# Hybrid encoder trunk on one core: gate and branch products with tokens on the partitions, and rounded activations and remainder in one 512-column step

## The chip, the cores and the metric

The kernel runs on one core of one Trainium2 chip. The metric is the device time in microseconds of one execution. The median of three runs of the kernel before is 993.6 us.

## The reference

Two layers work on 256 tokens of 1024 channels, all in float32. Each layer takes three mixers of the same input (differential attention, a gated DeltaNet scanned in both directions, windowed attention), gates and sums them, and then runs a gated feed-forward stage:

```python
z = x @ w_in                                   # gz: 3 x 1024 gate columns among them
proj = jnp.einsum('btnc,ncd->btnd', ys, w_branch)      # ys: three mixers, 512 wide
gates = jax.nn.sigmoid(gz.reshape(B, T, N_BRANCHES, D))
merged = jnp.sum(gates * proj, axis=2)
h = merged @ w_out;  x = layer_norm(DEEPNORM_ALPHA * x + h, ...)
gate, up = jnp.split(x @ w_up, 2, axis=-1)     # 2 x 2816 columns
gate = dwconv_centred(gate, conv_w) + conv_b   # width 3 over the tokens
f = (jax.nn.silu(gate) * up) @ w_down;  x = layer_norm(DEEPNORM_ALPHA * x + f, ...)
```

## The kernel before

**Three products for one.** TensorE multiplies in a rounded form of float32 (`F32R`). To keep the precision, each operand is split into a rounded part and a remainder (hi and lo), and `mm3` takes three products of each pair of tiles: hi*hi, hi*lo, lo*hi. The activations lie in `xTh` (rounded) and `xTl` (remainder), 8 tiles of 128 channels by 256 tokens each. The weights come from HBM in blocks of 512 KB (`raw`, 128x1024), ScalarE rounds a block (`hi`), VectorE takes the remainder (`lo`); `weights` and `take` do that, with 4 buffers of each kind.

**Two layouts.** `proj_ch` (and `pair`, which calls it) puts output channels on the partitions: the weights are stationary, the activations stream by, 256 columns in a step; a block of 128 output channels takes 8 x 3 steps of 256 columns. `token_major` and `proj_tok` put tokens on the partitions: the activations are stationary and 512 weight columns stream by. Before, the gates (`gz`, 24 blocks of 128 channels a layer), the branch products (`wb`, 12 blocks of 256 channels a layer), the feed-forward gate (`fg`, 22 blocks) and up (`fu`, 18 blocks) are of the first kind. `merge.product` makes the gates and branch products: a gate goes through Tanh on ScalarE, VectorE multiplies it with the branch product (`g_product<-g_product,mm_product`), adds the three branches, and splits the sum into hi and lo (`mh`, `ml`), which are stationary in `proj_tok("wo", ...)`.

**The feed-forward stage** goes over 11 groups `c` of 256 channels. A group makes `pg = pair("fg", l, c)` in one bank of PSUM, convolves it over the tokens (one affine step on ScalarE and two steps on VectorE for each of the two halves, read from PSUM), takes Silu, multiplies with `pu` (also in PSUM) and splits the result for `proj_tok("fd", ...)`. PSUM has 4 banks for such products (`mm`), 2 for the DeltaNet chain (`ch`), 2 for attention (`at`).

**The order** of the work is made at build time: `Plan` records all instructions with their dependencies, and a list scheduler with a table of costs sets the order on every engine. `ORDER` lists for each layer the products in the order in which they are asked for, `PRIO` shifts priorities. The gates and branch products stand in `ORDER` as fillers between the steps of the mixers. PE, VectorE and ScalarE each keep the order that results; a waiting instruction holds up all behind it on its engine.

Of the kernel before, what the change touches and what calls it, by code (L numbers as in the profile page):

```python
# [10 lines left out]
F32 = mybir.dt.float32  # L11
F32R = mybir.dt.float32r
F16 = mybir.dt.float16
U8 = mybir.dt.uint8
AF = mybir.ActivationFunctionType
# [35 lines left out]
PIECES = 2  # L51
PAIRS = ("s", "yc")
KEEP = {'wo': (4, ('D', 'N', 'x')), 'fd': ((4, ('g', 'g')), (4, ('g', 'g')))}
ORDER = [[('av', 0), ('ab', 0), ('k', 0), ('ak', 0), ('gz', 10), ('aq', 0), ('k', 1), ('q', 0), ('aq', 1), ('q', 1), ('ak', 1), ('gz', 1), ('v', 0), ('v', 1), ('gz', 0), ('gate', 0), ('gate', 1), ('cq', 0), ('wb', 1), ('ckv', 0), ('gz', 11), ('gz', 2), ('gz', 3), ('wb', 0), ('cq', 1), ('wb', 2), ('wb', 3), ('gz', 9), ('wb', 9), ('gz', 4), ('wb', 11), ('gz', 5), ('gz', 6), ('wb', 10), ('gz', 7), ('wb', 4), ('gz', 8), ('wb', 6), ('wb', 7), ('wb', 8), ('wb', 5)], [('av', 0), ('ab', 0), ('k', 0), ('ak', 0), ('gz', 10), ('aq', 0), ('k', 1), ('q', 0), ('aq', 1), ('q', 1), ('ak', 1), ('v', 1), ('gz', 0), ('gz', 3), ('v', 0), ('gate', 0), ('gate', 1), ('ckv', 0), ('gz', 1), ('cq', 0), ('wb', 1), ('wb', 0), ('gz', 11), ('gz', 2), ('cq', 1), ('wb', 2), ('gz', 9), ('wb', 3), ('gz', 4), ('wb', 9), ('wb', 11), ('gz', 5), ('gz', 6), ('wb', 10), ('wb', 4), ('gz', 8), ('gz', 7), ('wb', 6), ('wb', 7), ('wb', 8), ('wb', 5)]]


SIZES = {F32: 4, F32R: 4, F16: 2, U8: 1}
# [376 lines left out]
def _blocks(depth=DEPTH):  # L434
# [6 lines left out]
    for l in range(depth):  # L441
# [10 lines left out]
        for n in (0, 2, 1):  # L452
            for m in range(4):
                for b in range(2):
                    cols(("gz", l * 3 + n, 2 * m + b), "w_in", l, 4368 + n * D + (2 * m + b) * P, P)
                if n != 2:
                    cols(("wb", l, n, m), "w_branch", l, m * 256, 256, 4, sub=(n,))
                else:
                    sel = np.concatenate([g * 256 + t * 64 + np.arange(64) for t in range(4) for g in range(2)])
                    out.append((("wb", l, n, m), 4, 256, lambda i, l=l, m=m, sel=sel: i["w_branch"][l, 2][sel, m * 256:(m + 1) * 256]))  # L460
# [34 lines left out]
def tile_encoder_trunk(ctx: ExitStack, tc: tile.TileContext, a: dict, out: bass.AP, depth=DEPTH, tap=None):  # L495
# [884 lines left out]
    def merge(l, pr, ys, mh, ml):  # L1380
        gates, macc = {}, {}

        def product(nme, b):
# [18 lines left out]
            if nme != "wb":  # L1402
                return pair(nme, l, b)
# [102 lines left out]
```

## Time and profile before

| | |
|---|---|
| median of 3 runs | 993.6 us (992.38 to 994.38) |
| profiled execution, its time | 992.73 us |
| profiled execution, its span | 991.0 us |
| PE busy | 969.0 us (98%) |
| PE weight loads busy | 906.2 us (91%) |
| VectorE (DVE) busy | 722.3 us (73%) |
| ScalarE (ACT) busy | 588.8 us (59%) |
| GpSimd (POOL) busy | 73.0 us (7%) |
| mean HBM traffic | 166 GB/s |
| mean granted TensorE clock | 0.997 of full speed |

The span runs from the first to the last instruction; the execution's own time has 1.7 us more around it. Matmuls overlap: each record of a matmul is longer than the distance to the next one, and the sum of the records is more than the span, so the cost of a step is read from how many start in a stretch, not from its mean duration. A line of kernel.py is L195 for all instructions, as the recorder issues them, so rows are told apart by the names of tiles.

### The profile page before, as it was taken

How to read it: one execution, taken by the hardware profiler on the slowest of the kernel's cores; microseconds unless marked ns; L12 is line 12 of the kernel's file. 1: busy time of each engine (PE TensorE's matmuls, PEld its weight loads, DVE VectorE, ACT ScalarE, POOL GpSimd, SP SyncE). 2: the span in 40 equal slices, each digit the busy share in tenths (PEclk: the TensorE clock that was granted, in tenths of full speed). 3: DMA queues.
4: the chain of work that ended last, by engine and by line, in shares of the span. 5: the costliest groups of instructions: out<-in, count | busy, mean ns of one | idle time of the engine just before them, and what ended most of it. 6: DMA issues, size and time to landing. Idle time of an engine off the chain costs nothing.

```text
span 991.0 us, 19154 instructions
## 1 busy us (share of the span) xinstructions
PE 969.0 (98%) x7598; PEld 906.2 (91%) x7598; DVE 722.3 (73%) x1310; ACT 588.8 (59%) x1068; POOL 73.0 (7%) x84
## 2 busy tenths in 40 slices
PE   7999999999999999999999999999999999999996
PEld 6899999989988999988889999999899799999885
DVE  6799786665689766665688996966756995667555
ACT  5868966664455655553557787757744654555441
POOL 0520010100000100000005200000000010000000
PEclk9999999999999999999999999999999999999998
DMA  7644355464575655555635543425445855555661
GB/s 266 187 153 147 102 148 145 144 182 138 178 248 168 203 187 186 172 175 188 213 104 158 165 121 115 146 81 176 154 137 181 273 190 159 191 180 188 196 191 42
DMA packets 50109, 165.43 MB, mean 167 GB/s; under 512 B 5751, under 2 KB 11271, under 8 KB 50020
## 3 DMA queue, kind: packets, MB, share of 16 engines
q1 hardware_dynamic: 48644, 159.78, 50.9%
q0 software_dynamic: 1376, 4.43, 1.5%
q8 instruction: 59, 0.97, 0.4%
q14 instruction: 30, 0.25, 0.1%
HBM read 163.12 MB, written 1.07 MB: 166 GB/s over the span
## 4 chain that ended last, share of the span: by engine, by line
PE 81%; DVE 6%; ACT 4%; DMA 2%; POOL 1%; issue 1%; POOLq 0%; DVEq 0%; ACTq 0%
PE mm_proj_ch L195 48%; PE ch_run L195 6%; PE mm_product L195 6%; PE mm_run L195 6%; PE mm_token_major L195 3%; PE at_window L195 2%; PE at_attention L195 2%; PE ch_solve L195 2%; DMA raw_proj_tok<-in_w_dram 2%; PE ch_gdn L195 1%; ACT hi_take L195 1%; PE ch_scan L195 1%; DMA raw_take<-in_w_dram 1%; PE ch_finish L195 1%; POOL x_decay L195 1%
## 5 line engine op out<-in xcount | busy, mean ns | idle before, releaser
L195 PE MATMUL mm_proj_ch<-xTh,hi_take 128*128 128x256 f32 x1488 | 421.8, 286 | 0.9 <-ACT hi_take L195 0.5
L195 PE MATMUL mm_proj_ch<-xTl,hi_take 128*128 128x256 f32 x1488 | 420.2, 285 | 0.0
L195 PE MATMUL mm_proj_ch<-xTh,lo_take 128*128 128x256 f32 x1488 | 419.1, 285 | 0.0
L195 DVE TENSOR_TENSOR lo_take<-raw_take,hi_take 128x1024 fp32r<-128x1024 f32 x219 | 266.8, 1232 | 104.5 <-ACT hi_take L195 86.4
L195 ACT ACTIVATE hi_take<-raw_take 128x1024 fp32r<-128x1024 f32 x214 | 224.4, 1057 | 195.0 <-PE mm_proj_ch L195 136.5
L195 PEld LDWEIGHTS mm_proj_ch<-xTh,hi_take 128*128 128x128 f32 x1488 | 280.2, 189 | 3.5 <-ACT hi_take L195 1.8
L195 PEld LDWEIGHTS mm_proj_ch<-xTh,lo_take 128*128 128x128 f32 x1488 | 279.5, 189 | 2.8 <-issue 1.6
L195 PEld LDWEIGHTS mm_proj_ch<-xTl,hi_take 128*128 128x128 f32 x1488 | 280.2, 189 | 1.6 <-issue 0.8
L195 ACT ACTIVATE hi_proj_tok<-raw_proj_tok 128x1024 fp32r<-128x1024 f32 x50 | 52.8, 1060 | 66.8 <-PE mm_run L195 37.9
L195 DVE TENSOR_TENSOR lo_proj_tok<-raw_proj_tok,hi_proj_tok 128x1024 fp32r<-128x1024 f32 x50 | 61.0, 1223 | 42.9 <-ACT hi_proj_tok L195 42.9
L195 DVE SCALAR_TENSOR_TENSOR z_conv_silu<-mm_proj_ch,col_params,z_conv_silu 128x254 f32<-128x254 f32 (+1 forms) x96 | 39.1, 474 | 0.6 <-ACT z_conv_silu L195 0.5
L195 DVE SCALAR_TENSOR_TENSOR g_product<-g_product,mm_product 128x512 f32<-128x512 f32 x24 | 16.5, 686 | 24.5 <-PE mm_product L195 24.5
L195 POOL TENSOR_TENSOR s_tail<-s_tail,nhalf 128x1 f32<-128x1 f32 x8 | 5.3, 665 | 380.4 <-DVE s_tail L195 380.4
L195 ACT ACTIVATE e_window<-e_window,s_window 128x256 f32<-128x256 f32 x55 | 26.5, 498 | 10.5 <-DVE s_window L195 10.4
L195 PEld LDWEIGHTS <-h_solve 128*128 128x128 f16 x640 | 25.8, 98 | 4.2 <-ACT h_solve L195 0.4
L195 PE MATMUL mm_run<-hi_proj_tok,tile_encoder_trunk 128*128 128x512 f32 x88 | 27.5, 392 | 1.6 <-ACT tile_encoder_trunk L195 1.2
L195 PE MATMUL mm_run<-hi_proj_tok,ile_encoder_trunk 128*128 128x512 f32 x88 | 27.3, 391 | 0.0
L195 ACT ACTIVATE e_attention<-e_attention,s_attention 128x256 f32<-128x256 f32 x46 | 22.7, 503 | 5.3 <-DVE s_attention L195 5.1
L195 PE MATMUL mm_product<-ya_attention,hi_take 128*128 128x256 f32 x128 | 25.1, 287 | 0.0
L195 PE MATMUL mm_product<-ya_gdn,hi_take 128*128 128x256 f32 x128 | 23.7, 283 | 0.0
L195 PE MATMUL mm_product<-yc_window,hi_take 128*128 128x256 f32 x128 | 23.7, 283 | 0.0
L195 ACT ACTIVATE tile_encoder_trunk<-tile_encoder_trunk 128x512 f32<-128x512 f32 (+1 forms) x22 | 13.6, 625 | 16.6 <-DVE tile_encoder_trunk L195 16.6
(348 smaller groups left out, 1656.0 us busy)
## 6 DMA issues: line engine op xcount, KB each, us to landing
raw_take<-in_w_dram SPq DMA_DIRECT2D x226, 512.0 KB, 4.2
raw_proj_tok<-in_w_dram SPq DMA_DIRECT2D x60, 512.0 KB, 4.0
G_load_G<-band SPq DMA_DIRECT2D x24, 192.0 KB, 3.5
ya_ln_params<-in_lnp_dram POOLq DMA_DIRECT2D x16, 256.0 KB, 5.9
x<-in_xT_dram SPq DMA_DIRECT2D x4, 256.0 KB, 4.5
x<-in_x_dram SPq DMA_DIRECT2D x2, 512.0 KB, 4.6
out_dram<-x SPq DMA_DIRECT2D x8, 128.0 KB, 1.8
_tile_encoder_trunk<-in_w_dram SPq DMA_DIRECT2D x4, 128.0 KB, 3.7
```

Of the source, the lines that this page charges most:

```text
L195: op.ways.append((eng, lambda fn=fn, args=args, kw=kw: fn(*args, **kw), _cost(eng, name, outs, ins, args, kw), table))
```

## The change

It does four things. (1) The gate and branch weights are stored as blocks of 256 input rows by 512 output columns, and `merge.product` puts tokens on the partitions: the activations (or a mixer's output) are stationary and 512 weight columns stream by, for two halves of the tokens (`tt`) at once in two banks. (2) The gated sum then has tokens on the partitions, and four 128x128 transposes for each of 4 quarters a layer turn it back before it is split. (3) `xTh` and `xTl` become two halves of one tile `xT`, so that `wide` takes the steps hi*xTh and hi*xTl as one step of 512 columns; the two halves of the result are added afterwards by `halves_sum` (a copy by ScalarE or VectorE, and an addition on VectorE) into a buffer in SBUF, from which the rest of the stage reads. `wide` is used for `fg` and `fu` only. (4) `PRIO` and `ORDER` are new: `ORDER` has 6 gate and 6 product entries a layer instead of 12 and 12 (the long lists are left out below).

```diff
@@ _blocks
         for n in (0, 2, 1):
-            for m in range(4):
+            for h in range(2):
+                for b in range(KD // 2):
+                    cols(("gz", l * 3 + n, h, b), "w_in", l, 4368 + n * D + h * 512, 512, 2, b * 2)
                 for b in range(2):
-                    cols(("gz", l * 3 + n, 2 * m + b), "w_in", l, 4368 + n * D + (2 * m + b) * P, P)
-                if n != 2:
-                    cols(("wb", l, n, m), "w_branch", l, m * 256, 256, 4, sub=(n,))
...
+                    if n != 2:
+                        cols(("wb", l * 3 + n, h, b), "w_branch", l, h * 512, 512, 2, b * 2, sub=(n,))
...
-    xTh = cp.tile([P, KD, T], F32R, name="xTh")
-    xTl = cp.tile([P, KD, T], F32R, name="xTl")
+    xT = cp.tile([P, KD, 2, T], F32R, name="xT")
+    xTh, xTl = xT[:, :, 0], xT[:, :, 1]
...
+    def wide(key):
+
+        ps = ps_mm((P, 2, T))
+        hi, lo = take(key)
+        for j in range(KD):
+            TE.matmul(ps, hi[j], xT[:, j], start=j == 0, stop=False)
+            TE.matmul(ps[:, 0], lo[j], xTh[:, j], start=False, stop=j == KD - 1)
+        return ps
+
+    def halves_sum(out, ps):
+        A.copy(out, ps[:, 1])
+        V.tensor_tensor(out, ps[:, 0], out, op=ALU.add)
@@ merge.product
+            n, h = divmod(b, 2)
+            nk = KD if nme == "gz" else 4
+            pss = [ps_mm() for _ in range(2)]
+            for c in range(nk // 2):
+                w = take((nme, l * 3 + n, h, c if nme == "gz" else 1 - c))
+                for tt in range(2):
+                    ts = slice(tt * P, (tt + 1) * P)
+                    for j in range(2):
+                        if nme == "gz":
+                            lh, ll = xTh[:, 2 * c + j, ts], xTl[:, 2 * c + j, ts]
+                        else:
+                            lh, ll = [y[1 - c][:, j, ts] for y in ys[n]]
+                        mm3(pss[tt], lh, ll, w[0][j], w[1][j], c == j == 0, 2 * c + j == nk - 1)
             if nme == "gz":
-                n, m = divmod(b, 4)
-                ps = pair("gz", l * 3 + n, m)
-                gates[b] = buf("g", (P, 2, T))
-                S.activation(gates[b], ps, AF.Tanh, scale=0.5)
+                gates[b] = [buf("g") for _ in range(2)]
+                for tt in range(2):
+                    S.activation(gates[b][tt], pss[tt], AF.Tanh, scale=0.5)
                 return None
...
-                for j in (3, 2, 1, 0):
-                    mm3(ps[:, c], hi[j][:, cs], lo[j][:, cs], yh[j // 2][:, j % 2], yl[j // 2][:, j % 2], j == 3, j == 0)
...
+            for tt, gt in enumerate(gates.pop(b)):
+                V.scalar_tensor_tensor(gt, gt, 1.0, pss[tt], ALU.add, ALU.mult)
+                parts = macc.setdefault((h, tt), [])
+                parts.append(gt)
+                if len(parts) > 1:
+                    V.tensor_tensor(parts[0], parts[0], gt, op=ALU.add)
+                if len(parts) == 3:
+                    ps = ps_at((P, 4, P))
+                    for k in range(4):
+                        TE.transpose(ps[:, k], parts[0][:, k * P:(k + 1) * P], ident)
+                    h_, l_ = [buf(("z", "kk")[h], (P, 4, P), F32R) for _ in range(2)]
+                    S.activation(h_, ps, AF.Copy, scale=0.5)
+                    V.scalar_tensor_tensor(l_, ps, 0.5, h_.bitcast(F32), ALU.mult, ALU.subtract)
+                    mh[h, tt], ml[h, tt] = h_, l_
@@ feed-forward stage
-            pg = pair("fg", l, c)
+            pg = buf("h16", (P, 2, T))
+            for i in range(2):
+                ps = wide(("fg", l, 2 * c + i))
+                halves_sum(pg[:, i], ps)
...
-                pu = pair("fu", l, c)
+                pu = buf("h16", (P, 2, T))
+                for i in range(2):
+                    ps = wide(("fu", l, 2 * c + i))
+                    halves_sum(pu[:, i], ps)
```

**Place 1, PE in the feed-forward stage of the first layer.** `mm_proj_ch` and `mm_wide` are products in PSUM, `xTh`, `xTl` and `xT` the activations, `hi_take` and `lo_take` a weight block. Before, around the start of a new `fg` product:

```order
L195 MATMUL mm_proj_ch_33_804<-xTl,hi_take_81_809 128x256
L195 MATMUL mm_proj_ch_36_830<-xTh,hi_take_86_832 128x256
L195 MATMUL mm_proj_ch_36_830<-xTl,hi_take_86_832 128x256
L195 MATMUL mm_proj_ch_33_804<-xTh,lo_take_81_810 128x256
L195 MATMUL mm_proj_ch_33_804<-xTh,hi_take_81_809 128x256
```

With the change, at such a place:

```order
L195 MATMUL mm_wide_8_801<-xT,hi_take_77_803 128x512
L195 MATMUL mm_wide_8_801<-xT,lo_take_77_804 128x256
L195 MATMUL mm_wide_11_818<-xT,hi_take_80_820 128x512
L195 MATMUL mm_wide_13_829<-xT,hi_take_82_831 128x512
L195 MATMUL mm_wide_13_829<-xT,lo_take_82_832 128x256
```

Three steps of 256 columns became one of 512 and one of 256; each product now fills a bank of its own, and a second one is still begun before the first has its remainder of the weights.

**Place 2, VectorE at the same stage, one group of four weight blocks.** `e_...` is the convolved gate, `h_...` the new buffer of the added halves. Before:

```order
L195 TENSOR_TENSOR lo_take_101_895<-raw_take_104_893,hi_take_101_894 128x1024
L195 SCALAR_TENSOR_TENSOR e_tile_encoder_trunk_7_888<-mm_proj_ch_42_881,col_params_1_93,e_tile_encoder_trunk_7_888 128x255 x2
L195 TENSOR_TENSOR lo_take_102_901<-raw_take_105_899,hi_take_102_900 128x1024
L195 TENSOR_TENSOR lo_take_103_904<-raw_take_106_902,hi_take_103_903 128x1024
L195 TENSOR_TENSOR lo_take_104_909<-raw_take_107_907,hi_take_104_908 128x1024
L195 TENSOR_TENSOR e_tile_encoder_trunk_6_871<-mm_proj_ch_41_872,e_tile_encoder_trunk_6_871 128x512
L195 TENSOR_TENSOR N_tile_encoder_trunk_4_880<-e_tile_encoder_trunk_6_871,N_tile_encoder_trunk_3_879 128x512
```

With the change:

```order
L195 TENSOR_TENSOR lo_take_92_884<-raw_take_95_882,hi_take_92_883 128x1024
L195 TENSOR_TENSOR h_tile_encoder_trunk_7_870<-mm_wide_21_871,h_tile_encoder_trunk_7_870 128x256
L195 TENSOR_TENSOR D_tile_encoder_trunk_2_848<-e_tile_encoder_trunk_3_837,D_tile_encoder_trunk_1_847 128x512
L195 SCALAR_TENSOR_TENSOR e_tile_encoder_trunk_5_879<-h_tile_encoder_trunk_7_870,col_params_1_92,e_tile_encoder_trunk_5_879 128x255 x2
L195 TENSOR_TENSOR lo_take_93_888<-raw_take_96_886,hi_take_93_887 128x1024
L195 TENSOR_TENSOR h_tile_encoder_trunk_7_870<-mm_wide_22_875,h_tile_encoder_trunk_7_870 128x256
L195 TENSOR_TENSOR lo_take_94_895<-raw_take_97_893,hi_take_94_894 128x1024
L195 TENSOR_TENSOR h_tile_encoder_trunk_4_859<-mm_wide_19_860,h_tile_encoder_trunk_4_859 128x256
L195 TENSOR_TENSOR lo_take_95_899<-raw_take_98_897,hi_take_95_898 128x1024
L195 TENSOR_TENSOR h_tile_encoder_trunk_4_859<-mm_wide_20_864,h_tile_encoder_trunk_4_859 128x256
L195 TENSOR_TENSOR e_tile_encoder_trunk_4_858<-h_tile_encoder_trunk_4_859,e_tile_encoder_trunk_4_858 128x512
```

Behind each weight block there is one more addition of 128x256, and the convolution reads SBUF. Of the 80 copies that go before these additions, 73 stand on ScalarE and 7 on VectorE.

**Place 3, PE at the end of the first layer's mixers.** `mm_product` is a branch product, `mm_run` the first output projection (`wo`), `at_product` the new transposes, `tri` the identity. Before:

```order
L195 MATMUL mm_product_10_662<-ya_gdn_1_451,hi_take_66_660 128x256
L195 MATMUL mm_run_1_686<-hi_proj_tok_1_684,z_product_1_669 128x512
L195 MATMUL mm_run_1_686<-lo_proj_tok_1_685,z_product_1_669 128x512
L195 MATMUL mm_run_2_687<-hi_proj_tok_1_684,z_product_1_669 128x512
L195 MATMUL mm_run_2_687<-lo_proj_tok_1_685,z_product_1_669 128x512
L195 MATMUL mm_product_10_662<-ya_gdn_1_449,lo_take_66_661 128x256
```

With the change:

```order
L195 MATMUL mm_product_24_667<-hi_take_68_672,ya_gdn_1_458 128x512
L195 MATMUL mm_run_1_689<-hi_proj_tok_1_687,z_product_1_661 128x512
L195 MATMUL mm_run_1_689<-lo_proj_tok_1_688,z_product_1_661 128x512
L195 MATMUL mm_run_1_689<-hi_proj_tok_1_687,z_product_2_662 128x512
L195 MATMUL mm_run_2_690<-hi_proj_tok_1_687,z_product_3_664 128x512
L195 MATMUL mm_run_2_690<-lo_proj_tok_1_688,z_product_3_664 128x512
L195 MATMUL at_product_3_674<-tri,g_product_3_438 128x128 x4
L195 MATMUL mm_run_2_690<-hi_proj_tok_1_687,z_product_4_665 128x512
L195 MATMUL at_product_4_677<-tri,g_product_4_439 128x128 x4
```

(Rows between them that only repeat these are left out.) Eight steps of the output projection stand between the last branch product and the transposes that need it: the first half of the merged channels is ready earlier, and its steps fill that time.

## Rows read from the trace of the kernel before

**Rows 1.** The page, part 1: busy time, share of the span and number of instructions of PE, VectorE and ScalarE.

```profile
PE 969.0 (98%) x7598; PEld 906.2 (91%) x7598; DVE 722.3 (73%) x1310; ACT 588.8 (59%) x1068; POOL 73.0 (7%) x84
```

**Rows 2.** PE's waits for other engines: who waited, for whom, us in total, times, longest.

```profile
PE mm_proj_ch L195 <- ACT _tile_encoder_trunk L195: 5.5, 1, 5.5
PE mm_run L195 <- ACT tile_encoder_trunk L195: 1.2, 1, 1.2
PE mm_token_major L195 <- DVE xTl L195: 0.9, 2, 0.5
```

**Rows 3.** The chain of waits that ended last, pieces in order of time: start, length in us, engine, tile, number of instructions. Steps of 256 columns (`mm_proj_ch`, `mm_product`), of 512 (`ch_run`, `mm_token_major`), of 128 (`ch_finish`).

```profile
234.81 5.51 PE mm_product L195 x46
...
329.25 1.40 PE mm_token_major L195 x6
330.65 0.24 PE mm_proj_ch L195 x2
330.88 1.17 PE mm_token_major L195 x5
332.06 2.64 PE mm_proj_ch L195 x22
...
341.08 92.17 PE mm_proj_ch L195 x768
...
658.48 3.57 PE ch_finish L195 x32
...
827.09 19.99 PE mm_proj_ch L195 x168
...
951.89 29.93 PE ch_run L195 x132
```

**Rows 4.** Groups of instructions by tile and shape, the whole span: count, busy us, mean ns of one, idle time before and what ended it. Matmuls of the branch products (of three mixers, two of the rows of one shown), and the VectorE work on gates and products.

```profile
L195 PE MATMUL mm_product<-ya_attention,hi_take 128*128 128x256 f32 x128 | 25.1, 287 | 0.0
...
L195 PE MATMUL mm_product<-ya_attention,lo_take 128*128 128x256 f32 x64 | 18.1, 282 | 0.0
...
L195 DVE SCALAR_TENSOR_TENSOR g_product<-g_product,mm_product 128x512 f32<-128x512 f32 x24 | 16.5, 686 | 24.5 <-PE mm_product L195 24.5
L195 DVE TENSOR_TENSOR g_product<-g_product,g_product 128x512 f32<-128x512 f32 x16 | 11.0, 690 | 0.4
```

**Rows 5.** Busy time of each engine in the two steady stretches of the feed-forward stages: window, length, then PE, PE weight loads, DVE, ACT, POOL busy (number of instructions), granted clock, DMA share, GB/s.

```profile
345.00:430.00 85.00, 85.00 (x711) 85.00 (x710) 56.90 (x78) 46.73 (x60) 0.00 (x0) 1.00 0.58 188
840.00:920.00 80.00, 80.00 (x674) 80.00 (x673) 54.14 (x74) 44.42 (x58) 0.00 (x0) 1.00 0.58 186
```

**Rows 6.** Groups by tile and shape, the whole span: the nearest rows for the added work. An addition of 128x256 on VectorE; a copy from PSUM of 256 columns and one of 256 columns with a scale and a bias on ScalarE; a copy of 512 columns out of PSUM.

```profile
L195 DVE TENSOR_TENSOR xTl<-e_tail,xTh 128x256 fp32r<-128x256 f32 x24 | 9.1, 419 | 0.0
...
L195 ACT ACTIVATE tile_encoder_trunk<-mm_proj_ch,col_params 128x256 f32<-128x256 f32 x22 | 11.0, 552 | 0.0
...
L195 ACT ACTIVATE s_window<-mm_proj_ch 64x256 fp32r<-64x256 f32 x7 | 2.6, 376 | 0.1
...
L195 ACT ACTIVATE aT_window<-at_window 128x512 f32<-128x512 f32 x16 | 9.1, 591 | 2.4 <-PE at_window L195 2.4
```

**Rows 7.** Busy time by windows (columns as in rows 5): the heads of the two feed-forward stages, and the start of the second layer's mixers.

```profile
310.00:320.00 10.00, 10.00 (x81) 9.77 (x80) 9.96 (x19) 4.53 (x8) 0.00 (x0) 1.00 0.40 126
320.00:330.00 10.00, 10.00 (x81) 9.78 (x80) 9.94 (x17) 5.74 (x7) 0.00 (x0) 1.00 0.59 192
330.00:340.00 10.00, 10.00 (x68) 9.14 (x67) 4.02 (x6) 5.16 (x8) 2.70 (x5) 1.00 0.52 146
...
800.00:810.00 10.00, 9.85 (x79) 9.25 (x79) 9.97 (x20) 4.97 (x10) 1.66 (x3) 1.00 0.40 117
...
525.00:535.00 10.00, 9.57 (x66) 8.45 (x66) 9.48 (x10) 6.00 (x10) 10.00 (x7) 1.00 0.56 186
535.00:545.00 10.00, 9.51 (x80) 9.31 (x79) 5.90 (x8) 8.54 (x22) 3.19 (x6) 1.00 0.43 135
...
555.00:565.00 10.00, 9.44 (x78) 9.04 (x78) 9.77 (x17) 7.26 (x13) 4.70 (x3) 1.00 0.47 159
```

More of the change, by code (lines that the diff above doesn't have):

```diff
@@ L452, in _blocks @@
         for n in (0, 2, 1):
-            for m in range(4):
+            for h in range(2):
+                for b in range(KD // 2):
+                    cols(("gz", l * 3 + n, h, b), "w_in", l, 4368 + n * D + h * 512, 512, 2, b * 2)
                 for b in range(2):
-                    cols(("gz", l * 3 + n, 2 * m + b), "w_in", l, 4368 + n * D + (2 * m + b) * P, P)
-                if n != 2:
-                    cols(("wb", l, n, m), "w_branch", l, m * 256, 256, 4, sub=(n,))
-                else:
-                    sel = np.concatenate([g * 256 + t * 64 + np.arange(64) for t in range(4) for g in range(2)])
-                    out.append((("wb", l, n, m), 4, 256, lambda i, l=l, m=m, sel=sel: i["w_branch"][l, 2][sel, m * 256:(m + 1) * 256]))
+                    if n != 2:
+                        cols(("wb", l * 3 + n, h, b), "w_branch", l, h * 512, 512, 2, b * 2, sub=(n,))
+                    else:
+                        sel = np.concatenate([g * 256 + t * 64 + np.arange(64) for t in (2 * b, 2 * b + 1) for g in range(2)])
+                        out.append((("wb", l * 3 + n, h, b), 2, 512, lambda i, l=l, h=h, sel=sel: i["w_branch"][l, 2][sel, h * 512:(h + 1) * 512]))
         for half in range(2):
@@ L1395, in product @@
                 return ps
+            if nme not in ("gz", "wb"):
+                return pair(nme, l, b)
+            n, h = divmod(b, 2)
[8 more added lines that the diff above has]
+                            lh, ll = xTh[:, 2 * c + j, ts], xTl[:, 2 * c + j, ts]
+                        else:
+                            lh, ll = [y[1 - c][:, j, ts] for y in ys[n]]
+                        mm3(pss[tt], lh, ll, w[0][j], w[1][j], c == j == 0, 2 * c + j == nk - 1)
@@ L1396, in product @@
             if nme == "gz":
-                n, m = divmod(b, 4)
-                ps = pair("gz", l * 3 + n, m)
-                gates[b] = buf("g", (P, 2, T))
-                S.activation(gates[b], ps, AF.Tanh, scale=0.5)
-                return None
-            if nme != "wb":
-                return pair(nme, l, b)
-            n, m = divmod(b, 4)
-            yh, yl = ys[n]
-            gt = gates.pop(b)
-            hi, lo = take(("wb", l, n, m))
-            ps = ps_mm((P, 2, T))
-            for c in range(2):
-                cs = slice(c * P, (c + 1) * P)
-                for j in (3, 2, 1, 0):
-                    mm3(ps[:, c], hi[j][:, cs], lo[j][:, cs], yh[j // 2][:, j % 2], yl[j // 2][:, j % 2], j == 3, j == 0)
```

17 lines of the change are left out of this document (3 added, 14 removed).

## The prediction

> **What bounds the kernel now.** I read the busy times first. PE is busy for 969.0 of 991.0 us, VectorE for 722.3, ScalarE for 588.8 [rows 1]: one engine is nearly full, the others are not. The second view says whether PE waits for others: its three largest entries are 5.5, 1.2 and 0.9 us, the 5.5 us one wait [rows 2]. So there is hardly a wait to remove. The time can fall only if PE's own steps get cheaper or fewer, and it rises if a new wait stops PE.
>
> A busy PE has no idle time, so the price of a step has to come from elsewhere. The chain of waits gives stretches in which PE went from step to step: 92.17 us for 768 steps of 256 columns is 120.0 ns each, 19.99 for 168 is 119.0, and 5.51 for 46 of the branch products is 119.8. For 512 columns 29.93 us for 132 is 226.7 ns, and the two short stretches of `mm_token_major` give 233.3 (1.40 for 6) and 234.0 (1.17 for 5) [rows 3]. The records' own means, 282 to 287 ns for 256 columns [rows 4], are of no use here, since the records overlap. I take 119.5 ns for 256. One step of 512 is thus 4 to 13 ns cheaper than two of 256. All of the expected gain is in this difference.
>
> **The change part by part.** In the FFN products that become `wide`, there are 80 blocks (22 `fg` and 18 `fu` in each of two layers) of 8 tiles, 640 triples of steps. A triple was 3 x 119.5 = 358.5 ns. It becomes one step of 256 and one of 512; for the latter I take 230 ns, between the two kinds of row, since no row alternates the lengths for long. That saves 9.0 ns, 640 times: **-5.8 us**. Bounds: with 226.7 and 120.0 it is 13.3 ns (-8.5 us), with 234.0 and 119.0 it is 4.0 ns (-2.6 us).
>
> The gates were 48 blocks of 24 steps of 256, 1152 in all, and become 576 of 512. The activations are now stationary and weights stream, which is what `mm_token_major` does, so I take its 233: 2 x 119.5 - 233 = 6.0 ns, **-3.5 us** (13.3 ns at best, -7.7; 4.0 at worst, -2.3). The branch products go from 576 steps to 288. Here I take 119.8 from their own row and 227 from the other projection with tokens on the partitions: 12.6 ns, **-3.6 us** (12.9 ns at best, -3.7; with 234 it is 5.6 ns, -1.6).
>
> The transposes are new: 4 for each of 4 quarters and 2 layers, 32 steps of 128x128. A row of 32 such steps took 3.57 us, 111.6 ns each [rows 3]. PE is full, so they are paid: **+3.6 us**. The smallest sum of these four terms is -2.9, the largest -16.3, the chosen one -9.3.
>
> The Trainium skill (TensorE: Matmul & The Clock Gate, section "Back-to-back issue gap") speaks against this change: it gives the distance of two warm steps as their columns at 2.4 GHz plus 2.5 ns, so that joining two saves 2.5 ns. By that, 1504 joined pairs would be an estimated 3.8 us, which the transposes' 3.6 would eat up. The trace does not agree: its 256-column steps stand 119 to 120 ns apart, and the pair loses 4 to 13 ns.
>
> The clock stays out of it: it was granted in full (1.00, the 2.4 GHz level) in every stretch shown [rows 5, 7], and the new work leaves PE as full.
>
> *VectorE and ScalarE in the FFN stage.* Each block gets an addition of 128x256 from PSUM, nearest row 0.42 us, and a copy of 256 columns, nearest rows 0.376 and 0.552 us on ScalarE [rows 6]; 73 of the 80 copies stand on ScalarE. A group of four blocks is 32 triples, 96 steps, 11.5 us of PE now and 32 x 349.5 ns = 11.2 us afterwards. In the steady stretch VectorE is busy for 54.14 of 80 us and ScalarE for 44.42 [rows 5], so 7.75 and 6.4 us in a group. VectorE gets 4 x 0.42 (9.4 of 11.2), ScalarE 4 x 0.376 to 0.552 (up to 8.6). Both still fit, so I cost the 80 additions and copies at nothing. If the cover were gone, they would cost 80 x 0.42 = 34 us.
>
> The cover is thin at the heads of the two stages. VectorE is busy for 9.96 and 9.94 of 10 us at 310 to 330, and for 9.97 at 800 to 810 [rows 7]. Some 6 to 8 additions land there, 2.5 to 3.4 us a layer. They delay the next weight remainders, on which PE waits; but at 330 to 340 VectorE is busy for only 4.02 us, and much of its head work can be done then. Bounds: 0 to 6.7 us; I take **+1 us**, nearer to the free end because PE was at 10.00 through the same crowded stretches. Queued behind each addition on VectorE are the remainder of the next block and the convolution. They wait in addition for ScalarE's copy, which must not stand behind much else there.
>
> *PSUM.* Each `wide` takes one of four banks, and a bank comes free after copy and addition, about 1 us (0.591, a copy of twice the columns, plus 0.42) after 8 triples, 2.8 us. Four banks hold 11 us of products, enough.
>
> *The merge.* VectorE's products and additions keep number and size (24 and 16, 686 and 690 ns [rows 4]); Tanh likewise. What is longer is the end of the mixers: product, addition, transposes, ScalarE's split, VectorE's remainder, some 0.69 + 0.69 + 0.45 + 0.59 + 0.69 = 3.1 us [rows 4, 6] from the last branch product to the second half of `wo`. The order puts 8 `wo` steps (1.8 us) of the first half between, and the first half's remaining steps come on top. I cost it at nothing; with the cover gone it is 3.1 us a layer. SP's weight loads stay 512 KB a block and as many.
>
> **Sum.** -5.8 - 3.5 - 3.6 + 3.6 + 1.0 = **-8.3 us**. Against the profiled execution's 992.73 us this is 984.4. The median of the runs is 0.9 above that execution, so I predict **985.3 us**.
>
> **The rivals.**
>
> *A, the forecast* (0.61): PE stays the bound, and the steps bring what their lengths say. With the bounds of the steps' sum (-16.3 to -2.9) and no stall it is 977.3 to 990.7 us; the stall's own upper end of 6.7 on top of the worst steps would be 997.4, which I leave out of the range as two worst cases at once.
>
> *B, coarser fillers* (0.17). An entry of gates in the order was 48 steps of 256, 5.7 us of PE, and is now 48 of 512, 11.2 us. These entries fill the gaps of the DeltaNet and the attention. Where PE already misses work, at 525 to 565 in the second layer (9.57, 9.51, 9.44 of 10 us [rows 7]), a larger filler fits worse. If the cover for up to one old entry's length is missing in each layer, it costs 0 to 11.4 us; with half of that, 5.7, the time is 991.0. For it: half as many pieces to place. Against it: a list scheduler mixes the steps of several products, so the entry isn't the grain.
>
> *C, slower, VectorE becomes the bound in the FFN stage* (0.11). By the sums above 1.8 us of a group is left on VectorE. It is in order, and each addition stands behind a copy on ScalarE, which is itself in order. If VectorE idles for more than 1.8 us in a group, about 0.45 us at each of four additions, PE runs dry, and every further us costs 9 groups x 2 layers = 18 us. At 1 us over that is 985.3 + 18 = 1003 us; at 0.46 us over the gain is gone. For it: 99% busy at the heads. Against it: the order puts a whole remainder between additions, and ScalarE still has a quarter of its time free.
>
> *D, a larger gain* (0.07): the new order also removes PE's small waits and idle times in the middle, some us below A's low end, 970 to 977.
>
> *E, joining saves nothing* (0.04): a step costs by its columns alone, and the change does not do what it is for. The rows bear this out least: the smallest difference in them is 4 ns a pair, between 238 for two of 256 columns and 234 for one of 512 in the two short stretches of `mm_token_major` [rows 3]; the long stretches give 13. Between the low end of the sum and no saving at all the time is 991.7 (-2.9, +1) to 998.2 us (+3.6, +1), middle 995, hardly different from before. The rule of the Trainium skill (TensorE: Matmul & The Clock Gate, section "Back-to-back issue gap") comes to this case.
>
> **How the numbers follow.** A change under 0.2%, 2 us, can't be told from none here; that is 991.6 to 995.6 us. Faster: A (0.61), D (0.07), half of B (0.09): 0.77. Same: B 0.04, C 0.03, E 0.03: 0.10. Slower: B 0.04, C 0.08, E 0.01: 0.13. The range holds A and most of B: 977.0 to 992.5; D, C, E's upper part and the end of B (about 0.2) lie outside.
>
> **What would show it.** Right: PE still at 97% or more, its steps of `mm_wide` in the chain at 349 ns a pair, VectorE some 34 us busier than before, the granted clock unchanged, no wait of PE on the `h_` buffers. The gate steps at 233 ns and the branch steps at 227. Wrong: PE waiting on VectorE for `lo_take` in the FFN windows (C), PE's busy share falling in the DeltaNet stretches (B), or the 512-column steps at 239 ns (E).

## The result: 985.68 us, 0.8% faster

The changed kernel takes 985.68 us (median of 6 runs, 985.25 to 986.77) against 993.87 us for the kernel before in the same 6 rounds. The ratio is 0.9924, 95% interval [0.9913, 0.9934]; the forecast was 985.3 us. The profiled execution took 985.31 us, its span is 983.6 us against 991.0.

The busy times of the page's first part, to be read beside [rows 1]:

```profile
PE 961.5 (98%) x6126; PEld 829.6 (84%) x6126; DVE 759.4 (77%) x1404; ACT 605.8 (62%) x1134; POOL 75.1 (8%) x84
```

PE is as full as before, with 1472 steps fewer (1504 joined pairs, 32 transposes more); it is idle for 22.1 us (983.6 - 961.5) where it was for 22.0. VectorE is 37 us busier, ScalarE 17. PE's largest waits (who waited, for whom, us in total, times, longest), the answer to [rows 2]:

```profile
PE mm_proj_ch L195 <- ACT _tile_encoder_trunk L195: 5.9, 2, 4.9
PE mm_run L195 <- DVE tile_encoder_trunk L195: 1.4, 1, 1.4
PE mm_proj_ch L195 <- ACT hi_take L195: 1.1, 2, 0.8
PE mm_run L195 <- ACT tile_encoder_trunk L195: 1.0, 1, 1.0
```

The wait at the start is still the only long one. New is the second row: at the end of the first feed-forward stage PE waits for VectorE's last activations, 1.4 us where it waited for 0.4 before:

```profile
PE mm_run L195 <- DVE tile_encoder_trunk L195: 0.4, 1, 0.4
```

The chain of waits (start, length, engine, tile, number of instructions), which answers to [rows 3]:

```profile
218.99 54.55 PE mm_product L195 x235
273.55 0.44 PE at_product L195 x4
273.99 1.39 PE mm_product L195 x6
275.38 0.44 PE at_product L195 x4
275.82 5.49 PE mm_product L195 x24
281.31 1.82 PE mm_run L195 x8
283.13 0.44 PE at_product L195 x4
283.56 0.95 PE mm_run L195 x4
...
312.32 16.86 PE mm_wide L195 x96
...
334.30 95.47 PE mm_wide L195 x544
...
434.25 29.33 PE mm_run L195 x128
463.58 21.77 PE ch_run L195 x96
...
813.31 101.01 PE mm_wide L195 x576
```

544 steps of `mm_wide` are 272 pairs of one 512 and one 256, so 351.0 ns each; in the second stage 101.01 us for 288 is 350.7. The triples before were 360.0 and 357 to 359 in the same stages; the rows of the kernel before for its second stage, behind the one in [rows 3], are

```profile
847.19 22.96 PE mm_proj_ch L195 x192
...
870.26 22.84 PE mm_proj_ch L195 x192
...
893.21 28.30 PE mm_proj_ch L195 x238
```

Four transposes take 0.44 us, 110 ns each, and no gap stands beside them.

The windows (length, then PE, PE weight loads, DVE, ACT, POOL busy with counts, granted clock, DMA share, GB/s) that answer to [rows 5, 7]:

```profile
345.00:425.00 80.00, 80.00 (x458) 70.09 (x457) 65.55 (x101) 52.30 (x84) 0.00 (x0) 1.00 0.62 189
835.00:915.00 80.00, 80.00 (x459) 70.25 (x458) 68.28 (x108) 50.13 (x79) 0.00 (x0) 1.00 0.63 186
310.00:320.00 10.00, 10.00 (x57) 8.54 (x56) 9.96 (x21) 5.37 (x11) 0.00 (x0) 1.00 0.32 95
320.00:330.00 10.00, 10.00 (x58) 8.70 (x57) 9.11 (x17) 7.68 (x11) 0.00 (x0) 1.00 0.53 169
330.00:340.00 10.00, 10.00 (x53) 8.47 (x52) 8.65 (x21) 5.96 (x12) 2.70 (x5) 1.00 0.87 227
800.00:810.00 10.00, 9.31 (x48) 7.61 (x47) 8.07 (x13) 4.00 (x7) 1.85 (x4) 1.00 0.77 251
525.00:535.00 10.00, 10.00 (x78) 9.66 (x78) 9.86 (x14) 7.58 (x16) 6.74 (x8) 1.00 0.49 160
535.00:545.00 10.00, 10.00 (x62) 8.37 (x61) 9.80 (x18) 9.78 (x33) 3.71 (x5) 1.00 0.34 107
555.00:565.00 10.00, 10.00 (x133) 9.37 (x131) 10.00 (x25) 9.76 (x20) 0.00 (x0) 1.00 0.46 147
```

In the steady stretches PE stays at 80 of 80 us, and VectorE is at 82 and 85%. VectorE's work at 330 to 340 rose from 4.02 to 8.65 us, but only 0.8 of that are additions (two of them); the rest is other work that the new order has there. PE did not stop.

The groups for the added work (busy us, mean ns; then idle time before), which answer to [rows 6]: the additions of the two halves for half of the channel blocks, and the copies ahead of them on ScalarE.

```profile
L195 DVE TENSOR_TENSOR le_encoder_trunk<-mm_wide,le_encoder_trunk 128x256 f32<-128x256 f32 x40 | 16.7, 417 | 0.0
...
L195 ACT ACTIVATE le_encoder_trunk<-mm_wide 128x256 f32<-128x256 f32 x36 | 13.1, 365 | 0.0
```

### The profile page after: what moved, and what is told of

It reads as the page before. It is cut to its first block, busy times and chain, and to the rows that moved or that the text cites. A ratio compares the mean times of both kernels' runs of the same rounds, so it can differ in the third digit from the quotient of the medians.

```text
span 983.6 us, 16368 instructions
## 1 busy us (share of the span) xinstructions
PE 961.5 (98%) x6126; PEld 829.6 (84%) x6126; DVE 759.4 (77%) x1404; ACT 605.8 (62%) x1134; POOL 75.1 (8%) x84
## 4 chain that ended last, share of the span: by engine, by line
PE 83%; DVE 5%; ACT 4%; DMA 3%; issue 2%; POOL 2%; SPq 0%; POOLq 0%; ACTq 0%; DVEq 0%
PE mm_wide L195 23%; PE mm_product L195 19%; PE mm_proj_ch L195 15%; PE mm_run L195 7%; PE ch_run L195 6%; PE mm_token_major L195 3%; PE at_window L195 3%; PE ch_solve L195 2%; PE at_attention L195 2%; DMA raw_take<-in_w_dram 1%; ACT hi_take L195 1%; PE ch_gdn L195 1%; PE ch_finish L195 1%; PE ch_scan L195 1%; DVE lo_take L195 1%
## 5 line engine op out<-in xcount | busy, mean ns | idle before, releaser
L195 PE MATMUL mm_wide<-xT,hi_take 128*128 128x512 f32 x640 | 224.0, 394 | 0.1
L195 PE MATMUL mm_proj_ch<-xT,hi_take 128*128 128x256 f32 x928 | 177.8, 287 | 1.1 <-ACT hi_take L195 1.1
L195 PE MATMUL mm_wide<-xT,lo_take 128*128 128x256 f32 x640 | 178.3, 283 | 0.0
L195 PEld LDWEIGHTS mm_proj_ch<-xT,hi_take 128*128 128x128 f32 x928 | 144.7, 189 | 4.2 <-ACT hi_take L195 1.7
L195 PEld LDWEIGHTS mm_wide<-xT,hi_take 128*128 128x128 f32 x640 | 119.4, 188 | 26.6 <-DVE xT L195 0.3
L195 PE MATMUL mm_proj_ch<-xT,lo_take 128*128 128x256 f32 x464 | 133.4, 288 | 0.0
L195 PE MATMUL mm_product<-hi_take,xT 128*128 128x512 f32 x384 | 128.4, 403 | 0.0
L195 PEld LDWEIGHTS mm_wide<-xT,lo_take 128*128 128x128 f32 x640 | 120.4, 188 | 1.4
L195 PEld LDWEIGHTS mm_proj_ch<-xT,lo_take 128*128 128x128 f32 x464 | 87.6, 189 | 2.7 <-DVE lo_take L195 1.1
L195 PE MATMUL mm_product<-lo_take,xT 128*128 128x512 f32 x192 | 77.2, 402 | 0.0
```

Of the source, the lines that this page charges most:

```text
L195: op.ways.append((eng, lambda fn=fn, args=args, kw=kw: fn(*args, **kw), _cost(eng, name, outs, ins, args, kw), table))
```

## The experiments

Twelve runs, each against the kernel before on the same chip. Since the effects are a few us of 990, two readings are given: the ratio of the timed runs, and the profiled span beside the changed kernel's. The latter was profiled twice, 983.6 and 984.2 us, but the spans of its six timed executions lie between 983.5 and 985.1, so a single span is good to 1 to 2 us. Runs whose edit only changes what one planned instruction issues keep the planned order of everything else; that is said in each expectation. The edits are shown shortened.

Two things in the traces move a span and have nothing to do with an edit. The first 30 us, which no edit touches, differ by up to 1.5 us from one execution to the next; PE's wait at the start is 5.9 us in the changed kernel's and 4.9 to 5.2 in most others. And in some executions PE's clock was granted at the lower of its two levels, 1.2 GHz, for some steps behind PE's wait at the end of the first feed-forward stage, as here in the run with the merge's steps split (its chain, and a window):

```profile
435.58 30.93 PE mm_run L195 x128
```

```profile
436.00:439.00 3.00, 3.00 (x8) 2.32 (x8) 0.72 (x2) 0.00 (x0) 0.00 (x0) 0.50 0.08 31
```

The changed kernel had the same wait of 1.4 us, kept the full clock, and took 29.33 us for these 128 steps, so the lower clock cost 1.6 us. Apart from the run with two more additions, which pauses far more, four of the runs below had it (split merge, doubled transposes, one more addition, no addition), and the same four were 1.1 to 1.5 us ahead of the changed kernel after the first 30 us. The two nearly cancel: without both, the differences of their spans would be +5.0, +2.5, +11.0 and -0.5 us in place of the +5.4, +2.7, +11.5 and -0.4 given below.

**The price of the joined step in the feed-forward stage.**

```diff
-            TE.matmul(ps, hi[j], xT[:, j], start=j == 0, stop=False)
+            # planned as one step, issued as two
+            matmul(ps[:, 0], hi[j], xT[:, j, 0], start=j == 0, stop=False)
+            matmul(ps[:, 1], hi[j], xT[:, j, 1], start=False, stop=False)
```

> The changed kernel, with each 512-column step of the wide products issued as two steps of 256 columns at the same place of the same order; all else is kept. Theory (PE is the bound, the gain lies in the price of a step): a triple goes from the 351.0 ns of the changed kernel's chain (95.47 us for 272 pairs) back to 360.0 (92.17 us for 768 steps in the kernel before), 640 x 9.0 ns = +5.8 us, 991.5 us. Rival E, a step costs by its columns and joining saves 2.5 ns at most: +1.6 us or less, 985.7 to 987.3. Rival D, the gain came from the new order: no change, 985.7 us.

Measured: 988.47 us, ratio 0.9957 [0.9942, 0.9972]; span 986.8, +3.2 us. The joined step is worth something, and this much of the gain comes from it alone, so rival D's "no change" is out. But +3.2 is not +5.8. The windows of the `mm_wide` steps alone (columns as above, without POOL), first of this run, then of the changed kernel:

```profile
345.00:420.00 75.00, 75.00 (x635) 75.00 (x634) 11.70 (x28) 8.72 (x24) 1.00 0.63 190
```

```profile
345.00:420.00 75.00, 75.00 (x430) 65.71 (x428) 12.01 (x29) 8.74 (x24) 1.00 0.62 188
```

635 steps of 256 columns in 75 us (and the 0.28 us that the first record reaches in from the left) are 118.6 ns each, where the kernel before had 119.9 (628 of them, or 120.0 by its chain). A triple of such steps takes 356 ns, 5.0 more than a pair of the changed kernel, and 640 x 5.0 = 3.2 us, which is the whole of the difference. The other 4 ns a triple are not due to joining; what they are due to is looked into below.

**The price in the gates and branch products.**

```diff
-    mm3(pss[tt], lh, ll, w[0][j], w[1][j], ...)
+    # each of the three planned as one step, issued as two
+    for s in (slice(0, 256), slice(256, 512)):
+        matmul(ps[:, s], stationary, streamed[:, s], ...)
```

> The changed kernel, with each 512-column step of the gates and branch products issued as two of 256 columns with the same stationary tile, in the same order; transposes and the rest are kept. Theory: gates 576 x (240 - 232) ns = +4.6 us, branch products 288 x (240 - 228) ns = +3.5 us, together +8.1, 993.8 us. Rival E: 864 x 2.5 ns = +2.2 us at most, 987.9. Rival D (order): 985.7 us.

Measured: 988.60 us, ratio 0.9963 [0.9948, 0.9977]; span 989.0, +5.4 us. The chain of waits, the same stretch as the changed kernel's 54.55 us:

```profile
218.58 56.18 PE mm_product L690 x470
```

470 steps for 235, 119.5 ns each: a pair takes 239.1, one joined step 232.1. Taken apart by what is stationary, the joined gates' steps start 233.0 ns apart and their halves 118.6, a saving of 4.2 ns; for the branch products it is 228.4 against 2 x 119.8, 11.2 ns. 576 x 4.2 + 288 x 11.2 ns = 5.6 us, near what the span says. Rival E's 2.2 us at most is passed by the span and lies within the interval of the timed runs' difference (2.9 us by the medians); the distances of the steps decide for the theory.

**The transposes.**

```diff
-    TE.transpose(ps[:, k], parts[0][:, k * P:(k + 1) * P], ident)
+    for _ in range(2):
+        transpose(ps[:, k], parts[0][:, k * P:(k + 1) * P], ident)
```

> The changed kernel, with each of the 32 new transposes issued twice in a row; the rest is kept. Theory: PE is full at that place, so they are paid in full, 32 x 0.109 us = +3.5 us, 989.2 us. Rival: they lie in time in which PE would wait anyway for the chain at the end of the mixers, 0 to +1 us, 986 us.

Measured: 987.43 us, ratio 0.9941 [0.9928, 0.9953]; span 986.3, +2.7 us. Of their 3.5 us, 2.7 are paid by the span and 1.7 by the medians. At the first layer's mixers' end they are not hidden: in the chain above they stand in one row with PE's other steps.

**How much room VectorE has.** One and two more additions ahead of each of the 80, into a spare tile:

```diff
     def halves_sum(out, ps):
         A.copy(out, ps[:, 1])
+        V.tensor_tensor(spare, ps[:, 0], out, op=ALU.add)   # once, or twice
         V.tensor_tensor(out, ps[:, 0], out, op=ALU.add)
```

> The changed kernel, with one more addition of 128x256 from the same bank into a spare tile on VectorE ahead of each of the 80 additions of halves; the rest of the order is kept. 80 x 0.42 = 34 us more on VectorE. Theory (1.8 us of a group of 11.2 us were left on VectorE, and this takes 1.7): it nearly fits, 0 to +5 us, most at the crowded heads, 988 us. Rival C, VectorE already binds in this stage: the whole of it is paid, up to +34 us, 1019 us.

Measured: 996.76 us, ratio 1.0041 [1.0025, 1.0057]; span 995.1, +11.5 us, more than the theory's upper end and a third of the rival's. The steady stretches of this run:

```profile
340.00:420.00 80.00, 79.30 (x451) 68.92 (x450) 76.08 (x132) 53.21 (x82) 0.00 (x0) 1.00 0.62 189
835.00:915.00 80.00, 76.94 (x431) 65.88 (x431) 74.16 (x128) 47.40 (x73) 0.00 (x0) 1.00 0.57 175
```

VectorE stands at 95 and 93%, and PE at last falls below 80. The wait that was hidden is there:

```profile
PE mm_run L195 <- DVE tile_encoder_trunk L195: 1.9, 1, 1.9
PE mm_wide L195 <- ACT hi_take L195: 1.7, 4, 0.4
PE mm_wide L195 <- DVE lo_take L195: 1.5, 2, 0.8
...
PE mm_wide L195 <- DVE le_encoder_trunk L693: 0.7, 2, 0.5
```

PE waits for weights (`hi_take`, `lo_take`) that come late, in small pieces. It loses more in the second stage than in the first, and there it also waits, for 0.7 us, for additions that have not yet emptied a bank.

> The changed kernel, with two more additions into a spare tile ahead of each of the 80; order kept. VectorE then wants 9.4 + 3.4 = 12.8 us of a group that PE does in 11.2. Theory: VectorE is now the bound in the two stages, at least 1.6 us for each of some 20 groups, and it was full at 95% with one more: 12.8 / 0.95 - 11.2 = 2.3 us, +32 to +46 us, 1018 to 1032 us. Rival: the first extra addition's 11 us were a matter of waits in the order and not of VectorE's time; the second costs as much again, 1008 us.

Measured: 1033.29 us, ratio 1.0399 [1.0381, 1.0416]; span 1031.8, +48 us, just above the theory's upper end. The windows and the largest waits:

```profile
340.00:420.00 80.00, 74.14 (x393) 61.48 (x394) 76.75 (x144) 46.89 (x74) 0.00 (x0) 0.98 0.54 166
835.00:915.00 80.00, 69.54 (x372) 58.74 (x371) 75.34 (x140) 43.58 (x68) 0.00 (x0) 0.97 0.50 153
```

```profile
PE mm_wide L195 <- DVE le_encoder_trunk L693: 14.3, 10, 2.0
PE mm_wide L195 <- DVE lo_take L195: 5.4, 8, 1.4
```

VectorE stays at 94 to 96% though it has a third more to do in a group than in the changed kernel (12.8 us for 9.4): it is the bound. The largest wait is now that of `mm_wide` for the additions, for a bank that has not been emptied; with one more addition it was 0.7 us. PE now pauses, and its granted clock is below 1.00 too (0.98 and 0.97, means of the levels 2.4 and 1.2 GHz), which adds to the time. By the starts of the same steps in both traces, 36 of the 48 us are lost inside the two stages, 2.0 us in each of 18 groups, within the theory's 1.6 to 2.3; the other 12 are lost at the ends of the stages, where PE waits for the last activations and starts again at the lower clock.

Without the additions (planned, but nothing issued for them):

```diff
-        V.tensor_tensor(out, ps[:, 0], out, op=ALU.add)
+        plan.record(("DVE", "tensor_tensor", lambda *a, **k: None, (out, ps[:, 0], out), {}))
```

> The changed kernel without the 80 additions of halves (the copies stay, so the product of the rounded weights with the rounded activations is left out of what follows); the order of all else is kept. 34 us less on VectorE. Theory (VectorE has room, only its backlog at the heads and ends of the feed-forward stages costs): -1 to -2 us, 984 us. Rival, VectorE costs nothing at all: 985.5. Rival C, it already binds in the stage: -10 us or more.

Measured: 983.92 us, ratio 0.9909 [0.9894, 0.9923], beside 0.9910 for the changed kernel in its own repetition; span 983.2, -0.4 us. Its chain has the two long stretches of wide products:

```profile
333.22 95.47 PE mm_wide L195 x544
...
812.87 101.03 PE mm_wide L195 x576
```

With the additions they took 95.47 and 101.01 us, so inside the stages the additions cost nothing. PE's wait at the end of the first stage is 1.1 us in place of 1.4. Beside the changed kernel's first ratio, 0.9924, the gain would be 1.5 us and not 0.1; so the timed runs put the cost of the additions at 0 to 1.5 us and do not tell the rival "VectorE costs nothing" from the theory's -1 to -2, while the trace is nearer to the rival. Rival C is out.

**The changed kernel once more, and its steps in another sequence.**

> The changed kernel as it is, run beside the three that follow on the same chip, so that differences of a few tenths of a per cent can be read against it. All theories: ratio to the kernel before 0.992, 985 to 986 us.

Measured: 985.22 us, ratio 0.9910 [0.9895, 0.9925]; span 984.2.

```diff
         for j in range(KD):
             TE.matmul(ps, hi[j], xT[:, j], start=j == 0, stop=False)
+        for j in range(KD):
             TE.matmul(ps[:, 0], lo[j], xTh[:, j], start=False, stop=j == KD - 1)
```

> The changed kernel, with the eight 512-column steps of a wide product first and its eight 256-column steps of the weights' remainder behind them, in place of alternating; the order is planned anew. Theory (a step's price depends on its neighbours: 231 ns for a 512-column step between 256-column ones, 227 in a run of its own kind): 640 x 4 ns = -2.6 us, and the remainder is needed later, 983 us. Rival: the price is that of the operands, not of the neighbours: no change, 985.7 us, or worse by the new order.

Measured: 986.80 us, ratio 0.9929 [0.9914, 0.9943]; span 983.5. No gain. In the steady stretch the 512-column steps started 232.6 ns apart and the 256-column ones 119.0, in sum 351.7, as much as alternating (351.0). That a step is dearer because its neighbours are of another length is wrong. Its price goes with what it reads: steps of 512 columns that touch `xT`, whether streamed (`mm_wide`) or stationary (the gates, 233.0), take 231 to 233 ns; those with other operands take 227 to 229 (branch products 228.4; `mm_run` 29.33 us for 128, `ch_run` 21.77 for 96 in the chain above). Why, no run here tells.

**Where the other 4 ns of a triple come from.**

```diff
-            pg = buf("h16", (P, 2, T))
-            for i in range(2):
-                ps = wide(("fg", l, 2 * c + i))
-                halves_sum(pg[:, i], ps)
+            pg = pair("fg", l, c)              # likewise pu
```

> The changed kernel, with the feed-forward gate and up products made as before the change (three steps of 256 columns, no copy and no addition of halves, two products in one bank), but with xTh and xTl still in one tile; the order is planned anew with the new tables. Splitting the 512-column steps alone took a triple from 351 to 356 ns, not to the 360 of the kernel before. Theory 1, the other 4 ns come with the two halves of a bank (three steps in a row into the same columns cost more): triples are at 360 ns here, +5.8 us less the stall of the additions (0 to 1), about 991 us. Theory 2, they come with the layout of xT: triples at 356, +3.1 us less that stall, about 988 us.

Measured: 988.33 us, ratio 0.9950 [0.9936, 0.9964]; span 986.6. Steps took 119.7 and 119.5 ns in the two stages, triples 359.1 and 358.4, near theory 1 (the next run shows that these means are mixtures). So without `wide`, on top of everything else, the kernel is 2.4 to 4 us slower (0.9950 to 0.9910 in the ratios), not the 5.1 that 640 x 8 ns would make; a part of the saving went into waits (PE is idle for 21.3 us here and for 22.1 in the changed kernel).

```diff
         for j in range(KD):
-            TE.matmul(ps, hi[j], xT[:, j], start=j == 0, stop=False)
-            TE.matmul(ps[:, 0], lo[j], xTh[:, j], start=False, stop=j == KD - 1)
+            TE.matmul(ps[:, 0], hi[j], xTh[:, j], start=j == 0, stop=False)
+            TE.matmul(ps[:, 0], lo[j], xTh[:, j], start=False, stop=False)
+        for j in range(KD):
+            TE.matmul(ps[:, 1], hi[j], xTl[:, j], start=False, stop=j == KD - 1)
```

> The changed kernel, with the three products of a wide tile as steps of 256 columns, sixteen in a row into the first half of the bank and then eight into the second; the order is planned anew. In the steady stretch the triples took 356.0 ns where steps into the two halves alternated, and 358.8 where all three went into one. Theory 1, that difference comes from steps in a row into the same columns: 358 to 359 ns here, about 990 us. Theory 2, it comes from something else that the kernel without wide products has (two products in a bank): 356 ns, about 988 us.

Measured: 992.35 us, ratio 0.9988 [0.9976, 0.9999]; span 990.5. Both theories fall. The chain of waits has the two stages of this run in one row each:

```profile
336.03 96.84 PE mm_wide L195 x816
...
819.75 97.94 PE mm_wide L195 x816
```

It is the same code and the same sequence of operands, yet 118.7 ns a step in the first stage and 120.0 in the second. The starts show two beats: 118, 121, 120, 119, 115 ns over and over in the first stage, 117, 120, 123 in the second. A stretch keeps the beat that it has fallen into for long, but not for good: in the run without wide products the first stage goes at 120.0 until a step of 147 ns at 398 us, and at 118.7 behind it; the kernel before, in its second stage, goes over from 118.7 to 120.0 near 850 us without a late step, and back behind one of 143 ns at 863 us. Many late steps change nothing. So neither the target in PSUM nor the layout of `xT` is enough to explain the 4 ns: a run of 256-column steps goes at 118.7 or 120.0, and the kernel before happened to have the slower beat in its longest stretch. What sets the beat stays open.

**Wide products with the old order.**

> The kernel before, with xT in one tile and the wide products with their copies and additions alone; gates, branch products, order and priorities are those of before. Theory: -5.8 us for the triples and about +1 for VectorE's backlog, 993 - 5 = 988 us, the rest of the change being worth about 2.5 us (gates -2.3, branch products -2.9 by the split steps, transposes +2.7 by the doubled ones). Rival D, the new order carried the gain: less than 2 us here, 991 us or more.

```diff
-    xTh = cp.tile([P, KD, T], F32R, name="xTh")
-    xTl = cp.tile([P, KD, T], F32R, name="xTl")
+    xT = cp.tile([P, KD, 2, T], F32R, name="xT")
+    xTh, xTl = xT[:, :, 0], xT[:, :, 1]
...
-            pg = pair("fg", l, c)
+            pg = buf("h16", (P, 2, T))
+            for i in range(2):
+                ps = wide(("fg", l, 2 * c + i))
+                halves_sum(pg[:, i], ps)
+            # likewise pu; wide and halves_sum as in the change
```

Measured: 991.17 us, ratio 0.9974 [0.9961, 0.9987]; span 988.9, -2.1 us against the kernel before. The triples are at 351.1 and 350.7 ns, so 4.9 to 5.5 us cheaper, and some 3 us are lost elsewhere: PE's idle time is 24.6 us where it was 22.0. The window ahead of the second stage, first of the kernel before, then of this run:

```profile
780.00:790.00 10.00, 9.48 (x43) 7.62 (x43) 9.93 (x23) 6.41 (x11) 0.94 (x1) 1.00 0.80 264
```

```profile
780.00:790.00 10.00, 8.22 (x39) 6.35 (x38) 8.42 (x20) 5.73 (x11) 0.94 (x1) 1.00 0.83 255
```

PE loses 1.3 us more here. Of the rest, 0.8 us are at the end of the first stage and 0.6 at the head of the second, where the changed kernel is idle as well. The chain has a weight load in this window (kernel before, then this run):

```profile
783.51 4.75 DMA raw_take<-in_w_dram
```

```profile
780.19 6.99 DMA raw_take<-in_w_dram
```

ScalarE waits for the block, and PE for ScalarE's work behind it. This run was 2.2 us ahead of the kernel before up to here, the load ended only 1.1 us sooner, and 1.1 us of the lead were left. The last test asks whether the additions do it.

```diff
         A.copy(out, ps[:, 1])
-        V.tensor_tensor(out, ps[:, 0], out, op=ALU.add)
+        plan.record(("DVE", "tensor_tensor", lambda *a, **k: None, (out, ps[:, 0], out), {}))
```

> The kernel before with the wide products alone, as in the earlier run, but without the additions of halves (left out of the computation, the copies stay), order kept. With them the triples were 5.5 us cheaper but the run only about 2.5 us faster, and the stall at 780 to 810 us was larger. Theory, the additions on the crowded VectorE at the heads of the stages eat the rest: 3 us back, 988 us. Rival, it is the rearranged order and not the additions: no change, 991 us.

Measured: 989.93 us, ratio 0.9968 [0.9958, 0.9978]; span 988.4, -0.5 us. The 3 us of the theory do not come back; the 0.6 us between the two ratios lie within their intervals. But this span hides something: the wait at the start, ahead of any addition, was 1.3 us longer in this execution (first with the additions, then without):

```profile
PE mm_proj_ch L195 <- ACT _tile_encoder_trunk L195: 5.2, 1, 5.2
```

```profile
PE mm_proj_ch L195 <- ACT _tile_encoder_trunk L195: 6.5, 2, 5.7
```

PE's wait at the end of the first stage fell from 1.4 to 1.1 us. At 780 to 790 PE was at 9.14 us in place of 8.22:

```profile
780.00:790.00 10.00, 9.14 (x45) 7.17 (x44) 9.68 (x21) 6.60 (x13) 0.94 (x1) 1.00 0.83 265
```

```profile
780.99 5.67 DMA raw_take<-in_w_dram
```

But additions cannot be what costs PE there. The second stage's first wide product starts only at 800 us, and what differs in the chain is the weight load, 5.67 us this time. So the additions explain some tenths of a us of the loss, and the largest piece stands at a weight load. The changed kernel does not have that piece (PE is idle for 0.1 us between 750 and 800, where this order had 1.9 with the additions). Whether the new tables are the reason was not tried, since their entries are those of the new products.

## Why the prediction was right, and where it was off

| term | predicted | measured | from |
|---|---|---|---|
| wide products | -5.8 (-8.5 to -2.6) | -5.5 to -4.9 | triples of 360.0 and 357 to 359 ns became pairs of 351.0 and 350.7: 9.0 and 6.3 to 8.3 ns, each x 320; joining alone -3.2 |
| gates | -3.5 (-7.7 to -2.3) | -2.4 | 4.2 ns x 576 |
| branch products | -3.6 (-3.7 to -1.6) | -3.2 | 11.2 ns x 288 |
| transposes | +3.6 | +1.7 to +3.5 | doubled: medians 1.7, span 2.7; 110 ns each in the chain |
| stall on VectorE | +1 (0 to +6.7) | 0 to +1.5 | additions left out: span -0.4, ratios -0.1 or -1.5 |
| sum | -8.3 | -9.4 to -5.5 | span -7.4, medians -8.2 |

**The bound and the mechanism** were as predicted. PE stays at 98%, the gain is 1504 pairs that became single steps, each a few ns cheaper, and the split steps give it back (+3.2 and +5.4 us). Of the signs named, VectorE is 37 us busier (34 forecast), a pair of `mm_wide` stands at 351.0 and 350.7 ns (349), the clock is at 1.00, and no `mm_wide` waits for an addition. The end of the mixers, put at nothing, shows no wait in the first layer: the chain goes from branch products over transposes to `wo` without a gap.

**The prices.** The 512-column step was put at 230 in `wide` and 233 with the activations stationary, and came out at 230.7 and 233.0; the branch step was put at 227 and came out at 228.4. The nearest row, chosen by which operand is stationary, was the right choice: the gates went with `mm_token_major`, the branch products with `mm_run`. What was off is the other side of the subtraction: 119.5 ns for a 256-column step is a mean over two beats, 118.7 and 120.0, and the gates, whose halves run at 118.6, save 4.2 ns a step and not 6.0. In `wide` the term came out near its forecast, but joining is worth 3.2 us of it, 5.0 ns a pair and not 9.0; the rest is that the kernel before had the slower beat, which the rows that the forecast used contained without its being known. That part of the hit is luck. So is some of the sum: the gates and the branch products saved 1.5 us less than forecast, and the transposes and the stall cost less.

The Trainium skill (TensorE: Matmul & The Clock Gate, section "Back-to-back issue gap") gives its formula for an isolated step and says that a stream of weight loads and matmuls departs from it, which the prediction left out. Taken for a stream, as the prediction took it, it would have had 2.5 ns for each joined pair; the runs here do not agree: 5.0 in `wide`, 4.2 for the gates, 11.2 for the branch products.

**VectorE's room** (the cover of the 80 additions, and rival C) was right in its result and too generous in its margin. The predicted load of a group, 9.4 of 11.2 us, is 82 to 85% in the windows, as worked out. But not all of the remaining 1.8 us can be used: with 1.7 us more in each group PE already lost 11.5 us. VectorE did not get beyond 93 to 96% in the steady stretches of any run, so the point from which rival C decides is, as an estimate from these shares, about 0.95 x 11.2 - 9.4 = 1.2 us, not 1.8; no run tried that load. ScalarE's added copies took 365 ns, below both rows that bounded them.

**Rival B** (coarser fillers) did not come: PE is at 10.00 in the three windows where it was named, and its idle time as a whole is as before. PE lost a little at 800 to 810 (9.31 after 9.85) instead.

**Rival D** was put as small waits that the new order removes. The changed kernel's waits are about those of before (22.1 us of idle time, 22.0 before), while wide products in the old order add 2.6 us, half of it at a weight load ahead of the second stage. So there is no sign that the new tables add to the gain; they may be what keeps some of it, which is not shown.

## What to carry to other kernels

On a saturated engine, price a merged step as the difference of two measured step distances from rows whose operands are arranged alike, and check both sides: a ns in either is 0.6 us here for 640 steps. Do not count an engine that has to keep another one supplied as free up to 100%: between 85% and 95% of VectorE lay the whole way from "costs nothing" to "costs 11 us" here. Look for where a saving can be lost again: with the old tables half of it was, partly at a weight load that did not come sooner. And before two spans are compared, look at what the edit cannot have touched, here the wait at the start and the granted clock: each moved single spans by 1 to 1.6 us.

## What the runs showed of the hardware that was not expected

- A long run of 256-column steps goes at one of two even beats, 118.7 or 120.0 ns a step, and keeps it for long: 96.84 and 97.94 us for 816 steps of the same code in one run.
- A 512-column step that reads `xT`, on either side, takes 231 to 233 ns, others 227 to 229; with the 256-column steps alternating or behind it a pair takes 351.0 or 351.7 ns.
- Behind one and the same wait of PE the clock was granted in full in some executions and at 1.2 GHz for some steps in others: 29.33 and 30.93 us for 128 steps of 512 columns.
